# Longer visits for the projections of an RWKV-7 layer, and longer readiness times in its TensorE plan

## The chip, the cores and the metric

The kernel runs on one NeuronCore of a Trainium2 chip. The metric is the time of one execution on the device in microseconds (us), the median of several runs. Engines are named as the profile names them: PE is TensorE (matrix products), DVE is VectorE, ACT is ScalarE, POOL is GpSimd, and SP is SyncE, whose queue issues most of the DMA loads.

## The reference

A trunk of two layers over one sequence of 256 tokens and 1024 channels, all float32. Layer 0 mixes tokens by a bidirectional RWKV-7, layer 1 by dilated windowed attention; each is followed by a mixture of 32 experts of which a token uses two. The change lies in the RWKV layer, cut here to what matters:

```python
xs = h[:, :, None, :] + xx[:, :, None, :] * mu
rkv = jnp.einsum('bsjd,jde->bsje', xs[:, :, :3], w_rkv)      # r, k, v: 1024 x 1024 each
...
def step(state, inp):                                        # 16 heads of 64, two directions
    r_t, w_t, k_t, v_t, a_t, b_t = inp
    sa = jnp.einsum('bhvk,bhk->bhv', state, a_t)
    state = (state * w_t[:, :, None, :] + sa[:, :, :, None] * b_t[:, :, None, :]
             + v_t[:, :, :, None] * k_t[:, :, None, :])
    return state, jnp.einsum('bhvk,bhk->bhv', state, r_t)
...
y = (y - mean) * lax.rsqrt(var + RWKV_GN_EPS) * heads(ln_w) + heads(ln_b)
o = jnp.sum(heads(g) * (y + bonus), axis=0).reshape(bsz, s, d)
return jnp.einsum('bsd,de->bse', o, w_o)
```

## The kernel before

The RWKV layer works on blocks of 128 channels, that is two heads: eight blocks, i from 0 to 7. The sequence is cut into four chunks of 64 tokens, and the scan is turned into products within and between chunks. A block goes through these steps, each a generator whose `yield`s mark places where TensorE may turn to something else:

- `project` (L788): `keys` (L732) forms k and r (PE tile `kr`, 8 products each over the 8 blocks of input channels), `values` (L769) forms v (tile `v`, 8 products), `rates` (L747) the decay and the learning rate (tiles `ss` and `L`, then four tanh on ScalarE, L764, which empty the two `L` banks), `centred` the centred v (`vc`). The PSUM tiles of all of these, and of `yT`, `gT`, `ada` and the first half of `wo`, take turns in the two banks of the pool `pp`.
- `scale_keys` (L813) and `chunks` (L872): the decay sums, the products within chunks (`G`, masked on VectorE at L885), transposes (`BT`), `R2` and `sT`. At its end the block is "ready". The `project` of block i begins only when block i - 2 is "ready" (L790).
- `inverse` (L934): a 64 x 64 triangular inverse for each head, chunk and direction, in half precision (PE tile `iv`): six levels, each level two groups of 16 small products with a mask on VectorE (L979) or copies on ScalarE (L957) between them. Its first products are `iv<-cst,X`, its last `iv<-Q,E`.
- `recur` (L1015): four steps from chunk to chunk. A step is R (product with the state SD, an addition on VectorE at L1031), U (a product, copied on ScalarE at L1041), S (products, scaled into the new state SD on VectorE at L1057) and Y (the output, copied on ScalarE at L1073).
- `finish` (L1109): the normalisation on VectorE (with the reciprocal root in lines 345 to 354), the transposes `yT`, ScalarE's `yn` (L1124), the gate `gT` and the sum.

Beside them run `modulation_flow` (L1161), which forms the adaLN columns of later layers from streamed `aring` tiles (VectorE `acc`, L376; PE `ada`), and `outputs`, the output projection (`wo`): its first half (16 products over blocks 0 to 3) when block 7 is projected and block 3 is finished, its second half when the inverse of block 7 is done.

`weave` (L277) writes the order of the whole stage at build time, before anything runs. It keeps a time of its own. Each stream has a rank (`RANK`, L33: recurrence first, then inverse, ada, finish, chunks, supply of projections, outputs) and a time at which it may go on. `weave` takes the stream of the best rank whose time has come, advances its own time by an estimate of the products that it issued (`pe_work`) plus 0.12 where there were any, and lets the stream wait by the number that its `yield` gives. These numbers, the readiness times, stand for the work of VectorE and ScalarE until the next product has its data:

```python
ripe = [s for s in free if s[2] <= now]
s = min(ripe, key=lambda v: RANK[v[1]]) if ripe else min(free, key=lambda v: v[2])
...
r = next(s[0], "end")
...
used = pe_work[0] - before
now += used + (0.12 if used else 0.0)
s[2], s[3] = (now, r) if callable(r) else (now + (r or 0.0), None)
```

TensorE then executes its products in that order (`on_pe`, L261), and the other engines get priorities from the same time. The weights come through one SP queue: `wring` tiles of 128 x 2048 (two in the beginning), `aring` tiles of 128 x 1024 (two). When block 7 is projected and the ada columns are done, `releases` (L1280) frees the memory of the mixed inputs and of `aring` for four more `wring` tiles, then more when block 7 is ready, inverted and recurred; these fill with the first expert layer's weights.

Of the kernel before, what the change touches and what calls it, by code (L numbers as in the profile page):

```python
# [234 lines left out]
def trunk(ctx, tc, names, aps, out, stages=("rwkv", "moe0", "attn", "moe1"), dbg=None, ring=2):  # L235
# [12 lines left out]
    def bank(name="ps", tag="ps"):  # L248
        return psum[-1][tag].tile([128, 512], F32, name=name, tag=tag)
# [9 lines left out]
    pe_work, pinned = [0.0], [False]  # L259
# [77 lines left out]
    def col(i, n=1):  # L337
        t, i = (cols, i) if i < N_COLS else (cst_rw[0], i - N_COLS)
        return t[:, i:i + n]
# [243 lines left out]
    def rwkv(pool):  # L583
# [121 lines left out]
        def after(*what):  # L705
            return lambda: all(w in done for w in what if w[1] >= 0)
# [18 lines left out]
        def half(i):  # L725
            return slice(64 * i, 64 * i + 64)
# [5 lines left out]
        def keys(i):  # L732

            kr = stream.take(("kr", i)).rearrange("p (j k n) -> p j k n", j=2, k=KD)
            ps = bank(name="kr", tag="pp")
            for j, xs in enumerate((xk, xr)):
                for k in range(KD):
                    mm(ps[:, j * S:(j + 1) * S], kr[:, j, k, :], xs[k], start=(k == 0), stop=(k == KD - 1))
                    if k % 2:
                        yield  # L740
            krT = sup.tile([128, 2, S], F32, name="krT")
            A.activation(out=krT.rearrange("p j t -> p (j t)"), in_=ps, func=AF.Copy)
            sq = sup.tile([128, S], F32, name="ksq", bufs=1)
            A.activation(out=sq, in_=krT[:, 0], func=AF.Square, scale=col(C_KK + i))
            ws[i] = dict(sq=sq, kT=krT[:, 0], rT=krT[:, 1])
# [23 lines left out]
        def values(i, w):  # L769

            wv = w["vl"][:, 0:1024].rearrange("p (k n) -> p k n", k=KD)
            ps = bank(name="v", tag="pp")
            for k in range(KD):
                mm(ps[:, 0:S], wv[:, k, :], xv[k], start=(k == 0), stop=(k == KD - 1))
                if k % 2:
                    yield
            w["vT"] = sup.tile([128, S], F32, name="vT")
            A.activation(out=w["vT"], in_=ps[:, 0:S], func=AF.Copy)
# [9 lines left out]
        def project(i):  # L788

            yield after(("ready", i - 2))  # L790
            yield from keys(i)
            w = ws[i]
            w["vl"] = stream.take(("vl", i))
            yield
            yield from values(i, w)
            w["wait"] = 0.0
            g = rates(i, w)
            next(g)
            yield 0.2
            centred(i, w)  # L800
            yield 0.5
            for _ in g:
                yield
            done.add(("project", i))
# [67 lines left out]
        def chunks(i, w):  # L872
# [5 lines left out]
            for z in range(2):  # L878
                pair = [bank(name="G") for _ in range(2)]
                for c in range(4):  # L880
                    for hh, ps in enumerate(pair):
                        mm(ps[:, c * 128:(c + 1) * 128], BK[half(hh), z, c, :], AR[half(hh), z, c, :])
                for hh, ps in enumerate(pair):
                    for o, t in ((0, GV), (64, GI)):
                        V.tensor_tensor(out=t[:, z, hh].rearrange(aq, q=2),  # L885
                                        in0=ps.rearrange("p (a q n) -> p a q n", a=2, q=2)[:, :, :, o:o + 64],
                                        in1=mk[:, z, :, o:o + 64].unsqueeze(1).to_broadcast([128, 2, 2, 64]),
                                        op=ALU.mult)
                yield 1.6

            gv = GV.rearrange("p z h c n -> p (z h) c n")
            Ah, Al = A16[2 * (i % 2):2 * (i % 2) + 2]
# [122 lines left out]
        def recur(i, w):  # L1015
# [6 lines left out]
            for s in range(4):  # L1022
                cz = (s, 3 - s)
                if s == 0:
                    R = R2[:, 0]
                else:
                    R = odd.tile([128, 2, 64], F32, name="R", bufs=2)
                    ps = bank(name="R1", tag="ch")
                    for z in range(2):
                        mm(ps[half(1 - cz[z] % 2), 0:128], AR[:, z, cz[z], 0:64], ST[:, z, :])  # L1030
                    V.tensor_tensor(out=R, in0=ps[:, 0:128].rearrange("p (h n) -> p h n", h=2), in1=R2[:, s],  # L1031
                                    op=ALU.add)
                    yield 0.65
                ps = bank(name="U", tag="ch")
                for hh in range(2):
                    for z in range(2):
# [6 lines left out]
                if s < 3:  # L1043
# [16 lines left out]
                    pe_s = pe_work[0]  # L1060
# [12 lines left out]
                    A.activation(out=YT[h, z, cz[z] // 2, :], in_=py[h, 0:128], func=AF.Copy)  # L1073
                if s < 3:
                    ST = Sn
                    yield max(0.1, 0.9 - (pe_work[0] - pe_s))
                if s == 1:
                    done.add(("half", i))
            done.add(("recur", i))
# [29 lines left out]
        def finish(i, w):  # L1109
# [4 lines left out]
            sq = sub.tile([128, 8, 64], F32, name="gsq", bufs=1)  # L1114
            rs = head_scale(y, sq, 8)
            V.tensor_tensor(out=y, in0=y, in1=rs.unsqueeze(2).to_broadcast([128, 8, 64]), op=ALU.mult)
            yield 5.0
            ps = bank(name="yT", tag="pp")
            for z in range(2):
                for a in range(2):  # L1120
# [1 line left out]
                    tr(ps[:, o:o + 128], w["YT"][:, z, a, :])  # L1122
            y = sub.tile([128, 512], F32, name="yn", tag="gsq", bufs=1)
            A.activation(out=y, in_=ps, func=AF.Identity, scale=col(C_LNW + i), bias=col(C_LNB + i))  # L1124
            yield 0.1
            P.tensor_tensor(out=y, in0=y, in1=sT, op=ALU.add)
            V.tensor_tensor(out=y, in0=y, in1=w["gate"] if i == 6 else gate(i), op=ALU.mult)
            P.tensor_tensor(out=oT[:, i], in0=y[:, 0:S], in1=y[:, S:2 * S], op=ALU.add)
# [104 lines left out]
        for _ in keys(0):  # L1233
            pass
# [822 lines left out]
```

## Time and profile before

| | us |
|---|---|
| runs | 1192.64, 1196.88, 1201.08 |
| median | 1196.88 |
| the profiled execution's own time | 1199.42 |
| its span, first to last instruction | 1197.6 |
| PE busy | 1032.7 (86%) |
| DVE busy | 630.1 (53%) |
| ACT busy | 426.5 (36%) |

The span is what the trace covers; the profiled execution took 1.8 us more. Times in the rows below count from the start of the span. Busy times of PE are modelled, since products overlap. A float32 product stands in the trace as two records, so that `x4` in a timeline row is two blocks of a projection. Idle time in the trace is put down to the instruction that ended last of those waited for. PEclk is the clock that the chip granted to TensorE as a share of 2.4 GHz.

### The profile page before, as it was taken

The page shows a single profiled execution, that of the slowest core. Times are in us where ns is not written, and L with a number is a line of the kernel's source. Part 1 is how long each engine was busy: PE and PEld are TensorE (multiplying, and loading weights), DVE is VectorE, ACT ScalarE, POOL GpSimd, SP SyncE. Part 2 cuts the span into 40 slices and gives each one's busy share as a digit, 9 for nine tenths or more (in the row PEclk, how much of TensorE's full clock was granted, in tenths as well). Part 3 has the DMA queues.
Part 4 walks back from the last instruction along what each step waited for, and adds up shares of the span by engine and source line. Part 5 has one row for each costly group of instructions (what it writes and reads, how often), then busy time and mean ns, then how long its engine had stood idle before and what let it go on. Part 6 is the DMA issues. An engine that isn't in the chain of part 4 may idle for free. (4 is left out here: it accounts for less than half of the span.)

```text
span 1197.6 us, 24990 instructions
## 1 busy us (share of the span) xinstructions
PE 1032.7 (86%) x10564; PEld 689.1 (58%) x10564; DVE 630.1 (53%) x1438; ACT 426.5 (36%) x907; POOL 169.7 (14%) x122
## 2 busy tenths in 40 slices
PE   4769888989988999979988799898979999799876
PEld 3657666766666655434442388777858754344422
DVE  6873867577584446312211468987884762121112
ACT  3324456356446342101000367555544521010011
POOL 4410001010102700000000112122283000000000
PEclk8669999899979899989999999998989999899989
DMA  9453425234232766898999987876754589989995
GB/s 368 147 198 128 138 84 179 70 131 147 89 129 91 298 266 257 364 419 357 420 421 420 422 340 266 313 269 261 246 177 141 211 351 383 418 357 421 421 421 216
DMA packets 53197, 322.01 MB, mean 269 GB/s; under 512 B 5922, under 2 KB 6562, under 8 KB 21458
## 3 DMA queue, kind: packets, MB, share of 16 engines
q1 hardware_dynamic: 51986, 315.88, 67.8%
q0 software_dynamic: 800, 3.36, 0.7%
q8 instruction: 87, 1.43, 0.5%
q10 hardware_dynamic: 288, 1.05, 0.3%
q14 instruction: 36, 0.29, 0.1%
HBM read 319.22 MB, written 1.05 MB: 267 GB/s over the span
## 5 line engine op out<-in xcount | busy, mean ns | idle before, releaser
L271 PE MATMUL gu<-wring,xT 128*32 128x512 f32 x1024 | 132.2, 617 | 18.5 <-DMA wring<-in_w_moe_dram 11.2
L376 DVE SCALAR_TENSOR_TENSOR acc<-aring,silu,acc 128x512 f32<-128x512 f32 x140 | 115.0, 852 | 23.6 <-DMA aring<-in_w_ada_dram 23.3
L443 POOL TENSOR_TENSOR wl<-wring,wh 128x1024 f16<-128x1024 f32 x24 | 56.3, 2349 | 414.5 <-DMA wring<-in_w_qkv_dram 262.7
L271 PE MATMUL qkv<-hh,wl 128*128 128x256 f16 x384 | 106.7, 278 | 2.8 <-DVE wl L449 2.8
L271 PE MATMUL qkv<-hl,wh 128*128 128x256 f16 x384 | 106.6, 278 | 2.0 <-DVE hl L1720 2.0
L271 PE MATMUL qkv<-hh,wh 128*128 128x256 f16 x384 | 106.7, 278 | 1.6 <-ACT hh L1719 1.6
L271 PEld LDWEIGHTS gu<-wring,xT 128*32 128x32 f32 x1024 | 30.9, 112 | 101.9 <-issue 79.8
L271 PEld LDWEIGHTS <-wh 128*128 128x128 f16 x768 | 76.7, 100 | 13.3 <-issue 3.6
L271 PE MATMUL dn<-wring,hidT 128*32 128x256 f32 x1024 | 66.7, 410 | 18.1 <-ACT hidT L1522 18.1
L449 DVE SCALAR_TENSOR_TENSOR wl<-wring,wh 128x1024 f16<-128x1024 f32 x56 | 71.2, 1276 | 16.7 <-ACT wh L445 16.6
L271 PE MATMUL acc<-y,back 128*128 128x512 f32 (+1 forms) x144 | 65.9, 581 | 10.3 <-DVE y L1549 8.1
L271 PEld LDWEIGHTS xT<-oh,x 128*128 128x128 f32 x512 | 59.0, 192 | 21.1 <-issue 9.2
L445 ACT ACTIVATE wh<-wring 128x1024 f16<-128x1024 f32 x56 | 58.6, 1050 | 33.8 <-PE qkv L271 28.5
L1324 DVE SCALAR_TENSOR_TENSOR sg<-sg,gu 128x256 f32<-128x256 f32 x16 | 6.7, 420 | 118.2 <-ACT sg L1323 118.2
L1549 DVE TENSOR_TENSOR y<-dn,ga 128x512 f32<-128x512 f32 x28 | 19.4, 691 | 89.6 <-PE dn L271 60.4
L271 PE MATMUL xT<-oh,x 128*128 128x128 f32 x512 | 63.5, 280 | 2.5 <-DVE oh L1433 2.5
L271 PEld LDWEIGHTS dn<-wring,hidT 128*32 128x32 f32 x1024 | 32.3, 116 | 48.7 <-ACT hidT L1522 22.2
L1323 ACT ACTIVATE sg<-gu 128x256 f32<-128x256 f32 x16 | 6.1, 383 | 147.4 <-PE gu L271 147.4
L271 PE MATMUL qkv<-wl,hh 128*128 128x256 f16 x192 | 54.0, 281 | 0.0
L271 PE MATMUL qkv<-wh,hh 128*128 128x256 f16 x192 | 54.0, 281 | 0.0
L271 PE MATMUL qkv<-wh,hl 128*128 128x256 f16 x192 | 53.9, 281 | 0.0
L1465 ACT ACTIVATE back<-bT 128x256 f32<-128x256 f32 x16 | 6.2, 384 | 131.9 <-PE acc L271 131.9
(341 smaller groups left out, 2120.5 us busy)
## 6 DMA issues: line engine op xcount, KB each, us to landing
wring<-in_w_moe_dram SPq DMA_DIRECT2D x192, 1024.0 KB, 19.8
aring<-in_w_ada_dram SPq DMA_DIRECT2D x96, 512.0 KB, 4.5
wring<-in_w_qkv_dram SPq DMA_DIRECT2D x36, 1024.0 KB, 9.2
wring<-in_w_kr_dram SPq DMA_DIRECT2D x8, 1024.0 KB, 4.9
wring<-in_w_vl_dram SPq DMA_DIRECT2D x8, 640.0 KB, 4.8
wring<-in_w_rwo_dram SPq DMA_DIRECT2D x4, 1024.0 KB, 6.8
wring<-in_w_ato_dram SPq DMA_DIRECT2D x4, 1024.0 KB, 7.1
x<-in_x_dram POOLq DMA_DIRECT2D x2, 512.0 KB, 7.3
```

Of the source, the lines that this page charges most:

```text
L271: return on_pe(nc.tensor.matmul(out=o, lhsT=lhsT, rhs=rhs, start=start, stop=stop, **kw))
L376: V.scalar_tensor_tensor(out=acc[:, s], in0=w[:, s], scalar=silu[:, k:k + 1], in1=acc[:, s], op0=ALU.mult, op1=ALU.add)
L443: eng.tensor_tensor(out=lo, in0=src, in1=hi, op=ALU.subtract)
L445: A.activation(out=hi, in_=src, func=AF.Copy, scale=by)
L449: V.scalar_tensor_tensor(out=lo, in0=src, scalar=by, in1=hi, op0=ALU.mult, op1=ALU.subtract)
L1323: A.activation(out=o, in_=ps[:, 0:256], func=AF.Tanh, scale=0.5)
L1324: V.scalar_tensor_tensor(out=o, in0=o, scalar=1.0, in1=ps[:, 0:256], op0=ALU.add, op1=ALU.mult)
L1465: A.activation(out=back, in_=ps[:, 0:S], func=AF.Copy)
L1549: V.tensor_tensor(out=y, in0=py[c], in1=gates[i, 5][:, c * 512:(c + 1) * 512], op=ALU.mult)
```

## The change

Four kinds of lines change, and nothing of what is computed:

- `keys` and `values` offer TensorE to others after every fourth block of input channels instead of every second.
- `project` waits 1.6 after its start condition.
- Seven readiness times grow: between the parts of `chunks` 1.6 becomes 2.4; in `recur` the time behind R 0.65 becomes 0.85 and the time behind Y 0.9 becomes 1.1; in `finish` 5.0 becomes 7.0 ahead of `yT` and 0.1 becomes 1.2 ahead of `gT`.

```diff
             for j, xs in enumerate((xk, xr)):
                 for k in range(KD):
                     mm(ps[:, j * S:(j + 1) * S], kr[:, j, k, :], xs[k], start=(k == 0), stop=(k == KD - 1))
-                    if k % 2:
+                    if k % 4 == 3:
                         yield
...
                 mm(ps[:, 0:S], wv[:, k, :], xv[k], start=(k == 0), stop=(k == KD - 1))
-                if k % 2:
+                if k % 4 == 3:
                     yield
...
         def project(i):

             yield after(("ready", i - 2))
+            yield 1.6
             yield from keys(i)
...
-                yield 1.6
+                yield 2.4
...
-                    yield 0.65
+                    yield 0.85
...
-                    yield max(0.1, 0.9 - (pe_work[0] - pe_s))
+                    yield max(0.1, 1.1 - (pe_work[0] - pe_s))
...
-            yield 5.0
+            yield 7.0
             ps = bank(name="yT", tag="pp")
...
-            yield 0.1
+            yield 1.2
             P.tensor_tensor(out=y, in0=y, in1=sT, op=ALU.add)
```

The numbers steer `weave`, so the order of TensorE's products changes through the whole stage. Three places show how. In the rows that follow, the number at the start is the place in the engine's order, and x gives how many equal instructions stand in a row. First TensorE in the recurrence of block 0, before:

```order
765 L271 MATMUL kr<-xr,wring 128x256 x2
766 L271 MATMUL U<-R,TT 64x64 x4
767 L271 MATMUL R_1315<-vc,GV 64x64 x16
768 L271 MATMUL sT<-bb,cstr 128x256 x2
769 L271 MATMUL S<-SD_359,cst 64x128 x2
770 L271 MATMUL S<-UV,BT 64x64 x4
771 L271 MATMUL Y<-SD_359,AR 64x128 x2
772 L271 MATMUL Y<-UV,GI 64x64 x4
773 L271 MATMUL kr<-xr,wring 128x256 x2
774 L271 MATMUL R_1359<-SD_360,AR 64x128 x2
```

And the same place of the recurrence now (`R<-vc,GV` is the product R2 of block 1):

```order
758 L271 MATMUL v<-xv,wring 128x256 x4
759 L271 MATMUL U<-R,TT 64x64 x4
760 L271 MATMUL R_1330<-vc,GV 64x64 x16
761 L271 MATMUL sT<-bb,cstr 128x256 x2
762 L271 MATMUL S<-SD_359,cst 64x128 x2
763 L271 MATMUL S<-UV,BT 64x64 x4
764 L271 MATMUL Y<-SD_359,AR 64x128 x2
765 L271 MATMUL Y<-UV,GI 64x64 x4
766 L271 MATMUL v<-xv,wring 128x256 x4
767 L271 MATMUL R_1380<-SD_360,AR 64x128 x2
```

The visits between the steps hold four blocks instead of two, and the projection of block 2 is further on: it is at v instead of r. Second, TensorE behind the rate products of block 4, before:

```order
2558 L271 LDWEIGHTS Ah_355
2559 L271 MATMUL iv<-T_3138,Ah_355 64x64
2560 L271 MATMUL L<-hidw,wring 128x256 x2
2561 L271 MATMUL L<-hida,wring 128x256 x2
2562 L271 MATMUL kr<-xk,wring 128x256 x2
2563 L271 LDWEIGHTS X_3140
```

Now the rate products of block 4 stand at 2126, and the first visit to the projection of block 5 at 2434:

```order
2125 L275 MATMUL BT<-cst,BK 128x128 x4
2126 L271 MATMUL L<-hidw,wring 128x256 x2
2127 L271 MATMUL L<-hida,wring 128x256 x2
2128 L271 LDWEIGHTS E_2739
...
2433 L271 MATMUL iv<-T_3022,Ah_355 64x64
2434 L271 MATMUL kr<-xk,wring 128x256 x4
```

The next projection no longer follows at once; the rows between are those of the inverse (a weight load and a product each), the chunks and the recurrence. Third, SP's queue from the load of block 6's v weights to the first expert weights, before:

```order
36 L153 DMA wring<-in_w_vl_dram 128x1280
37 L153 DMA aring<-in_w_ada_dram 128x1024 x4
38 L153 DMA wring<-in_w_kr_dram 128x2048
39 L153 DMA aring<-in_w_ada_dram 128x1024 x4
40 L153 DMA wring<-in_w_vl_dram 128x1280
41 L153 DMA aring<-in_w_ada_dram 128x1024 x2
42 L153 DMA wring<-in_w_rwo_dram 128x2048 x4
43 L153 DMA wring<-in_w_moe_dram 128x2048 x45
```

And now:

```order
34 L153 DMA wring<-in_w_vl_dram 128x1280
35 L153 DMA aring<-in_w_ada_dram 128x1024 x2
36 L153 DMA wring<-in_w_kr_dram 128x2048
37 L153 DMA aring<-in_w_ada_dram 128x1024 x6
38 L153 DMA wring<-in_w_vl_dram 128x1280
39 L153 DMA wring<-in_w_rwo_dram 128x2048
40 L153 DMA aring<-in_w_ada_dram 128x1024 x2
41 L153 DMA wring<-in_w_rwo_dram 128x2048
42 L153 DMA aring<-in_w_ada_dram 128x1024 x4
43 L153 DMA wring<-in_w_rwo_dram 128x2048 x2
44 L153 DMA wring<-in_w_moe_dram 128x2048 x45
```

The last six ada loads have moved behind all the projections' weights and between the loads of the output weights. From the transposes `zT` behind the last RWKV outputs on, TensorE's order is the same in both kernels.

## Rows read from the trace of the kernel before

**Rows 1.** Stage windows: PE, PEld, DVE, ACT, POOL busy us (xinstructions), PEclk, DMA share, GB/s
```profile
95.00:415.00 320.00, 287.34 (x4461) 216.33 (x4459) 207.62 (x524) 160.46 (x355) 52.13 (x42) 0.94 0.38 131
415.00:481.00 66.00, 60.54 (x731) 35.30 (x731) 33.64 (x126) 21.78 (x58) 1.99 (x2) 0.98 0.67 264
481.00:680.00 199.00, 172.17 (x1393) 78.02 (x1386) 40.23 (x99) 23.58 (x70) 0.00 (x0) 0.97 0.98 406
```

**Rows 2.** Waits of PE from 95 to 415: total us, times, longest us
```profile
PE kr L271 <- ACT at L764: 5.4, 4, 1.7
PE R L271 <- DVE SD L1057: 3.8, 5, 1.1
...
PE yT L275 <- DVE rsq L352: 2.7, 1, 2.7
PE U L271 <- DVE R L1031: 2.1, 4, 1.0
...
PE yT L275 <- DVE rsq L353: 1.7, 1, 1.7
PE gT L271 <- ACT yn L1124: 1.7, 3, 0.7
...
PE yT L275 <- ACT at L764: 0.8, 1, 0.8
```

**Rows 3.** Timeline of PE: start us, us, engine, line, product, shape, xcount [idle before]
```profile
103.18 1.13 PE L271 MATMUL kr<-xr,wring 128*128 128x256 f32 x4
104.24 0.44 PE L271 MATMUL iv<-T,Ah 64*64 64x64 f16 x16
104.61 1.99 PE L271 MATMUL kr<-xr,wring 128*128 128x256 f32 x8
106.53 0.44 PE L271 MATMUL iv<-Q,X 64*64 64x64 f16 x16
106.81 0.42 PE L271 MATMUL iv<-X,Q 64*64 64x64 f16 x16
```

**Rows 4.** Timeline of PE, the start of a projection at 161
```profile
161.31 1.13 PE L271 MATMUL kr<-xk,wring 128*128 128x256 f32 x4 [1.73 <-ACT at L764]
```

**Rows 5.** Timeline of ACT, the tanh of line 764 ahead of it
```profile
160.80 0.47 ACT L764 ACTIVATE at<-L,a0h 128x256 f32<-128x256 f32 x1
```

**Rows 6.** Timeline of PE, steps of the inverse and the recurrence in the tail
```profile
424.23 0.44 PE L271 MATMUL iv<-Q,X 64*64 64x64 f16 x16
...
425.57 0.44 PE L271 MATMUL iv<-T,Ah 64*64 64x64 f16 x16 [0.28 <-ACT T L957]
...
426.79 0.44 PE L271 MATMUL iv<-Q,X 64*64 64x64 f16 x16 [0.52 <-DVE Q L979]
...
441.09 1.12 PE L271 MATMUL wo<-wring,oT 128*128 128x512 f32 x2
442.14 0.45 PE L271 MATMUL U<-R,TT 64*64 64x64 f32 x8
442.96 0.63 PE L271 MATMUL S<-UV,BT 128*64 128x64 f32 x8 [0.37 <-ACT UV L1041]
...
444.38 0.44 PE L271 MATMUL R<-SD,AR 128*64 128x128 f32 x4 [0.55 <-DVE SD L1057]
445.29 0.45 PE L271 MATMUL U<-R,TT 64*64 64x64 f32 x8 [0.47 <-DVE R L1031]
```

**Rows 7.** Short windows around falls of the clock, columns as in rows 1
```profile
205.00:209.00 4.00, 4.00 (x41) 2.96 (x40) 3.69 (x7) 2.38 (x5) 2.10 (x2) 0.57 0.07 26
248.00:252.00 4.00, 2.60 (x22) 1.52 (x22) 4.00 (x16) 3.12 (x7) 0.00 (x0) 0.72 0.79 269
326.00:330.00 4.00, 4.00 (x80) 3.36 (x77) 0.95 (x2) 2.95 (x8) 0.00 (x0) 1.00 0.01 4
332.00:340.00 8.00, 5.27 (x73) 4.48 (x70) 6.03 (x28) 4.27 (x10) 0.34 (x1) 0.50 0.45 133
```

**Rows 8.** Window from the first expert load to the first expert product, columns as before
```profile
385.00:481.00 96.00, 85.97 (x1071) 53.33 (x1073) 50.19 (x161) 34.67 (x84) 23.45 (x18) 0.95 0.69 274
```

## The prediction, made before the changed kernel ran

> **What bounds the kernel now.** I read the stage windows first. They cut the span where the code cuts it: the woven RWKV stage, its tail up to the first expert product at 480.8 us, the first expert layer, and the rest [rows 1]. In the expert layer the DMA share is 0.98 at 406 GB/s, while TensorE is idle for 27 of 199 us: the layer runs at the pace of its weights, and it ends a fixed time after it starts. The program from the last RWKV output on stands in the same order in both kernels, so the change is worth what it moves the start of the expert layer by, and nothing else.
>
> Before that start the DMA has room (0.38), VectorE is busy for 207.6 of 320 us and ScalarE for 160.5. TensorE is busy for 287.3 of 320, and takes its products strictly in the order that the planner wrote. So its time there is made of four things: the products, what a change from one kind of product to another costs, the waits (320.0 - 287.3 = 32.7 us), and the clock, whose mean of 0.94 over 320 us means that some 19 us of full clock are missing. The waits of TensorE then say which of them come from an order that is too early for its data [rows 2]: kr on the tanh that frees its bank 5.4 us, yT on the normalisation 2.7 + 1.7 + 0.8 = 5.2, R on the state 3.8, U on R 2.1, gT on yn 1.7. These five make 18.2 us, and five of the change's longer readiness times stand just there. They add no wait to any instruction: they only move it back in TensorE's order.
>
> **A: fewer visits.** Both kernels execute the same products. A visit of two blocks takes from 103.18 to 104.24, which is 1.06 us to the next product; one of four takes from 104.61 to 106.53, 1.92 us [rows 3]. Two visits of two cost 2.12, so each visit that goes saves 0.20 us. The inverse step beside it takes 0.37 us when a projection follows (104.24 to 104.61) and 0.28 when another inverse step follows (106.53 to 106.81), so up to 0.09 more. In the order there are 78 visits by kr and v from block 1 on before (six of them of four blocks already) and 42 after: 36 x 0.20 = 7.2 us, at most 36 x 0.29 = 10.4, and nothing if TensorE only waits longer instead. I take -7.2, as TensorE is 90% busy.
>
> **B: waits that are aimed at.** The wait for the bank: kr stands at 161.31 after 1.73 us of idle, and the tanh that releases the bank starts at 160.80 and takes 0.47, so it ends at 161.27 [rows 4, 5]. The added 1.6 us ahead of a projection covers all but about 0.1 of each such wait: -5.0. The 5.0 that became 7.0 covers the two shorter yT waits and 2.0 of the longest: -4.5. For gT 0.1 became 1.2, more than any of its three waits: -1.7. R gets 0.2 more on each of 5 waits, -1.0; U 0.2 on each of 4, -0.8. Sum -13.0. The lower bound is -18.2, all of it; the upper is 0, if no product is ready to stand in the gap. I take -13.0 because a planner that holds a product back puts another stream's product there, and through most of the stage there is one. The sixth, in the chunks, meets none of the larger waits [rows 2]; I cost it at nothing, as inverse and recurrence products fill it. Without them it would cost the 0.8 that it adds, 6.4 us over eight blocks.
>
> **C: new waits.** Fewer, larger pieces of projection run out sooner. After block 4's last rate product the order before goes straight on to the next projection; the new order has some 300 rows of inverse and recurrence in between, since block 5 has to wait for "ready" of block 3. Such windows follow blocks 4, 5, 6 and 7, and one stands at the end of the first output half: five. What a wait costs there, the tail shows. With no filler at all one recurrence step lasts from 442.14 to 445.29, of which 0.37 + 0.55 + 0.47 = 1.39 us are waits; where inverse and recurrence alternate, 425.57 to 426.79 has 0.28 + 0.52 = 0.80 [rows 6]. High end: all four steps bare in five windows, 4 x 5 x 1.39 = 27.8 us. Low end 0. In the new order the two chains alternate in these windows, as they do in the second of these rows, so I take 5 x 0.80 = +4.0.
>
> **D: output products that move.** With the projections gone earlier, 12 instead of 5 of the first output's blocks stand ahead of the last block's inverse, and 4 instead of 11 inside it. Seven times 1.05 us (441.09 to 442.14 [rows 6]) = 7.4 us are paid earlier and leave the tail. Whether the tail gives them back depends on what they hid there: products of the inverse behind copies on ScalarE and masks on VectorE. That inverse runs from 415 to 442 with its outputs in it; without seven of them it would take 19.5 us. An inverse step waits for its mask at least until 1.22 us after the product ahead of it (425.57 to 426.79), and the half of a level that goes through ScalarE takes 1.34 (424.23 to 425.57): five levels are 12.8 us, by estimate, which leaves 6.7 us for its first and last parts, unbounded by these rows. So much of it can come back. The bounds are 0 and +7.4; I take about half, +3.4.
>
> **E: the clock.** The clock falls to its lower level, 1.2 GHz, in stretches. Two of them follow waits that B removes: 205 to 209 at 0.57, behind waits of yT and gT, and 248 to 252 at 0.72, in the wait of kr [rows 7]. They lose 4 x 0.43 + 4 x 0.28 = 2.8 us, and I take -2.8. But the longest fall, at 0.50 from 332 on, follows a stretch in which TensorE was busy for 4.00 of 4.00 us. The Trainium skill ("TensorE: Matmul & The Clock Gate", the section "HAM oscillation — how this bites in real kernels") puts such falls down to gaps in which the engine waits; by it, removing waits would bring back most of the 19 us and the sum would be some 16 us lower. The trace agrees at 205 and 248 and not at 330, so that is a rival below. The bounds are -19 (full clock throughout) and +20 (five windows of 8 us at half clock, each losing 4, the size of the row from 332 to 340).
>
> **What hides the rest.** The queue of loads has the projections' weights behind other ada loads than before (six ahead of the last vl). Before, too, a run of six stands ahead of one projection load, and TensorE shows no wait for a DMA in the stage; the DMA share of 0.38 [rows 1] is the cover. If it went, v would wait for its load of 128 x 1280 floats, 0.66 MB or 1.6 us at the expert layer's 406 GB/s. A shorter stage loads VectorE more: 207.6 us of work over about 305 is 68%, still cover.
>
> **The sum.** -7.2 - 13.0 + 4.0 + 3.4 - 2.8 = -15.6 us. The profiled execution took 1199.4 us (span 1197.6 and 1.8 around it), so 1183.8; it lies 2.5 us above the median of 1196.9, which makes **1181**.
>
> **The rivals.**
> Waits only move (0.20). Each product held back leaves a gap, or what stands in it makes the next chain late. B and E are then 0, and -7.2 + 4.0 + 3.4 is 0.2: 1197. For it: the longer waits are in the planner's own time, and most waits end on VectorE or ScalarE, whose speed doesn't change. Against it: 5.4 us hang on one bank at a fixed delay.
> The clock holds (0.12). With few waits the clock stays at 2.4 GHz: E is -19, the sum -31.8: 1165. For it the falls at 205 and 248, against it the one from 332.
> The weights come late (0.06). The extra ring space for expert weights opens after the last ada product, which stood some 300 rows of the order ahead of the last inverse and now stands some 40 ahead of it. Up to 481 the queue brought in 96 x 274 = 26.3 MB [rows 8], 65 us at the expert layer's 406 GB/s; from the start of the last inverse to the expert layer there were 66 us, and will be some 62. With two gaps of 4 us the layer starts 8 us short of weights: 1189.
> Fillers run out: slower (0.12). All windows of C are bare, 27.8, the clock falls in each, +20, and the outputs give nothing back, +7.4: with A and B +35 us, 1232. It decides from the point at which C, D and E together exceed 20 us for slower at all, 32 for slower by over 1%. For it: the new order's long rows of small products; against it: alternating chains at 425 hardly waited.
>
> **How the numbers follow.** A measurement of this kernel tells about 1% (12 us) from no change. My forecast has 0.50; its own range is 1173 to 1190, and 0.40 of the 0.50 lies below 1185. Faster: 0.40 + 0.12 = 0.52. Within 1%: 0.10 + 0.20 + 0.06 = 0.36. Slower: 0.12. The range from 1165 to 1198 takes in the clock's rival and the one in which waits only move, and leaves out the slow case and a little beyond the other end.
>
> **What would show it.** Right: the kr wait on the tanh near 0.5 us in all, yT and gT nearly gone, four-block visits of about 1.92 us, the first expert product near 465 us and the expert layer still 199 us long. Wrong in C: waits of R, U and S above 12 us in all. Wrong in D: a last inverse that still takes 25 us. Wrong in E: a mean clock below 0.92 ahead of the tail. Wrong as a whole: a first expert product later than 480, or an earlier one with an expert layer longer by as much.

## The result, and the profile after

The changed kernel takes 1203.1 us (median; 1196.5 to 1209.2) where the kernel before took 1194.6 on the same chip. The ratio is 1.0076 with a 95% interval from 1.0049 to 1.0103: slower by three quarters of a per cent, where 1.3% faster was predicted. One of the eleven executions took 5376.42 us and counts in neither the spread nor the ratio. The profiled execution took 1209.15 us (span 1207.4), 9.7 us more than that of before; it is the longest of the other ten, so its rows show one to three microseconds more than the median loses.

First the stage windows of the changed kernel, with the columns of [rows 1], cut at the same events: the last inverse's start, the first expert product (492.06 us, where the prediction named "later than 480" as its sign of being wrong as a whole) and the end of the first expert layer.

```profile
95.00:424.00 329.00, 290.70 (x4471) 222.91 (x4469) 217.57 (x523) 158.37 (x353) 51.25 (x42) 0.92 0.38 127
424.00:492.00 68.00, 58.09 (x721) 35.48 (x715) 33.47 (x126) 22.43 (x60) 1.98 (x2) 0.90 0.66 255
492.00:691.00 199.00, 172.64 (x1387) 77.80 (x1388) 40.42 (x100) 23.19 (x68) 0.00 (x0) 0.95 0.98 404
```

The expert layer lasts 199 us, as in [rows 1], and starts 11.3 us later (480.80 before). So the loss lies where the prediction looked for the gain. One window over the whole stage, of the kernel before and then of the changed one, splits it:

```profile
95.00:480.80 385.80, 347.68 (x5185) 251.48 (x5183) 241.06 (x648) 182.24 (x413) 54.13 (x44) 0.95 0.43 154
```

```profile
95.00:492.06 397.06, 348.78 (x5184) 258.39 (x5182) 251.10 (x648) 180.80 (x413) 53.23 (x44) 0.92 0.42 149
```

TensorE is idle for 397.06 - 348.78 = 48.3 us instead of 38.1, so 10.2 of the 11.3 us are waits. Its busy time did not fall by the 7 us of the saved visits; the granted clock is 0.92 instead of 0.95 in the same stretch. And VectorE, with the same 648 instructions, is busy 10 us longer. That last number points at the cause, but does not measure the loss: the visits alone, which are faster than before, have it too (250.3 us of VectorE up to their first expert product). The waits of TensorE in the same stretch, to be held against [rows 2]:

```profile
PE iv L271 <- DVE T L999: 10.6, 3, 6.8
PE R L271 <- DVE SD L1058: 6.4, 7, 2.3
PE iv L271 <- DVE Q L980: 5.7, 8, 1.9
PE U L271 <- ACT TT L1012: 4.2, 3, 2.2
...
PE S L271 <- ACT UV L1042: 2.2, 2, 1.8
...
PE U L271 <- DVE R L1032: 0.8, 1, 0.8
PE yT L275 <- DVE YT L1117: 0.6, 1, 0.6
```

Three of the five waits that the change aimed at are gone: kr 5.4 to nothing (1.7 us of the wait for that bank now stand at an ada product), gT 1.7 to nothing, yT 5.2 to 0.6. Of the other two, U on R fell from 2.5 to 0.8 and R on the state rose from 4.3 to 6.4 (the values of before up to 480.8 us). The largest is a new one, for T of line 999, which VectorE makes at the end of each inverse; before, TensorE did not wait for it at all. Here is the longest of the three, on TensorE, then VectorE, then POOL, each a timeline of the changed kernel:

```profile
401.93 0.44 PE L271 MATMUL iv<-X,E 64*64 64x64 f16 x16
409.14 0.64 PE L271 MATMUL iv<-X,cst 64*64 64x512 f16 x2 [6.77 <-DVE T L999]
```

```profile
397.01 0.42 DVE L886 TENSOR_TENSOR GV<-G,cstr 128x256 f32<-128x256 f32 x1 [0.84 <-PE G L271]
...
400.17 0.69 DVE L1128 TENSOR_TENSOR yn<-yn,gT 128x512 f32<-128x512 f32 x1 [1.73 <-POOL yn L1127]
408.06 0.43 DVE L899 TENSOR_TENSOR Ah<-Ah,cst 128x512 f16<-128x512 f16 x1 [7.21 <-POOL Al L898]
408.41 0.68 DVE L999 TENSOR_TENSOR T<-iv,E 128x512 f16<-128x512 f32 x1
```

```profile
395.18 3.73 POOL L566 TENSOR_TENSOR wring<-wring,ga 128x512 f32<-128x512 f32 x3
398.86 1.27 POOL L1127 TENSOR_TENSOR yn<-yn,sT 128x512 f32<-128x512 f32 x1
400.09 4.94 POOL L566 TENSOR_TENSOR wring<-wring,ga 128x512 f32<-128x512 f32 x4
404.97 1.15 POOL L898 TENSOR_TENSOR Al<-GV,Ah 64x512 f16<-64x512 f32 x1
406.08 0.72 POOL L1129 TENSOR_TENSOR oT<-yn 128x256 f32<-128x256 f32 x1
406.88 1.15 POOL L898 TENSOR_TENSOR Al<-GV,Ah 64x512 f16<-64x512 f32 x1
```

Read from the bottom: POOL gates the rows of the output projection, 16 multiplications of 1.23 us or more each (L566, called by `outputs`). `Al` of block 7 stands behind them. VectorE takes its instructions in the order of these rows: the addition to `Ah` waits 7.21 us for `Al`, and T of block 6's inverse, which does not read that `Al`, stands behind `Ah`. TensorE waits 6.77 us for T. In VectorE's order of the changed kernel `Ah` stands ahead of the running inverse's T in three of eight blocks, in the kernel before in none. That was theory 1.

### The profile page after: what moved, and what is told of

It is laid out like the page before. It is cut to its first block, busy times and chain, and to the rows that moved or that the text cites. A ratio compares the mean times of both kernels' runs of the same rounds, so it can differ in the third digit from the quotient of the medians.

```text
span 1207.4 us, 24980 instructions
## 1 busy us (share of the span) xinstructions
PE 1035.4 (86%) x10564; PEld 697.1 (58%) x10564; DVE 641.7 (53%) x1438; ACT 424.2 (35%) x907; POOL 168.5 (14%) x122
## 3 DMA queue, kind: packets, MB, share of 16 engines
q10 hardware_dynamic: 288, 1.05, 0.3%
HBM read 319.22 MB, written 1.05 MB: 265 GB/s over the span
## 5 line engine op out<-in xcount | busy, mean ns | idle before, releaser
L566 POOL TENSOR_TENSOR wring<-wring,ga 128x512 f32<-128x512 f32 x32 | 45.6, 1454 | 64.2 <-DMA wring<-in_w_rwo_dram 34.8
```

Of the source, the lines that this page charges most:

```text
L566: P.tensor_tensor(out=wk[:, j, s], in0=wk[:, j, s], in1=gate[:, s], op=ALU.mult)
```

## The experiments

Every ratio is against the kernel before, run beside it on the same chip, in five rounds; the intervals are of 95%. One table first, as the pieces are read against each other. "Gate moved" takes the 16 multiplications off POOL, "Al moved" the two subtractions per block.

| Order of TensorE | POOL as it is | gate moved | Al moved | both moved |
|---|---|---|---|---|
| before | 1 | 1.0014 (e9) | 0.9896 (e5) | 0.9931 (e12) |
| visits only | 0.9929 (e1) | 0.9940 (e14) | 0.9933 (e7) | |
| project wait only | 1.0087 (e8) | 0.9994 (e10) | | |
| all readiness times, no visits | 1.0037 (e2) | | | |
| visits and project wait | 1.0115 (e6) | | | |
| changed, without project wait | 0.9955 (e4) | | 0.9948 (e16) | |
| changed, finish times of before | | 0.9989 (e15) | | |
| changed | 1.0076 | 0.9980 (e11) | 0.9967 (e3) | 0.9922 (e13) |

### First set: which half, and is it T?

e1 has the visits alone (`k % 4 == 3` in `keys` and `values`), e2 the readiness times alone (the other lines of the diff), and e4 is the changed kernel without one of them:

```diff
             yield after(("ready", i - 2))
-            yield 1.6
             yield from keys(i)
```

e3 is the changed kernel with Al moved:

```diff
-                P.tensor_tensor(out=l, in0=a, in1=h, op=ALU.subtract)
+                V.tensor_tensor(out=l, in0=a, in1=h, op=ALU.subtract)
```

> Edit: the kernel before with only the two visit sizes changed (four blocks of channels), all readiness times as before. In its order VectorE has the next block's addition to Ah ahead of the El of the running inverse in three of the eight inverses (none in the kernel before). Theory 1 (the larger visits bring the next block's chunks forward, and their VectorE and POOL work then stands in in-order queues ahead of the end of the running inverse): the waits of TensorE for the DVE tile T of L998 come back, 6 us or more in sum, and what the saved switches give (7 us) is lost again: 1.000 to 1.010 times before. Rival 2 (the readiness times do the harm, the visits are worth what was predicted): 0.993 to 0.997, with those waits near 0.

Measured: 0.9929 [0.9901, 0.9958]. The waits for T were 3.6 us, neither the 6 of theory 1 nor the 0 of rival 2, and the visits alone are worth what the prediction's term A said. The time is at the lower edge of rival 2's, and theory 1's count of `Ah` ahead of T does not decide: this kernel has three as well.

> Edit: the kernel before with only the readiness times changed (all six), visits of two blocks as before. Its VectorE order has no Ah ahead of an El. Theory 1 (visits bring the chunks forward): the waits for the DVE tile T are 0, the aimed-at waits kr, yT and gT are gone as in the changed kernel, and the time is 0.990 to 1.000 of before. Rival 2 (the readiness times do the harm, through waits of R, U and S and a lower clock where the fillers were used up): 1.005 to 1.013, with the waits of R, U and S over 12 us as in the changed kernel.

Measured: 1.0037 [1.0015, 1.0060], between the two. kr is gone and no wait for T appears, and yT still has 1.7 us and gT 0.5; but iv on Q takes 10.1 us in place of 3.6, and iv on ACT's T 6.8 in place of 1.9.

> Edit: the changed kernel with the subtraction Al (two instructions per block) moved from POOL to VectorE, so that the addition to Ah has no wait for POOL in VectorE's queue. Theory 1: the waits of TensorE for the DVE tile T fall from 10.6 us to under 4 us, and with the clock that falls after them the time is 6 to 12 us under the changed kernel's, 0.997 to 1.003 of before. Rivals 2 and 3 (R, U and S waits, or the clock where fillers lack): the waits for T may fall, but the time stays within 3 us of the changed kernel's, 1.005 to 1.010 of before.

Measured: 0.9967 [0.9942, 0.9992], 1.1% under the changed kernel; the waits for T fell from 10.6 to 4.3. That is close to what theory 1 asked for (under 4), but a control was missing.

> Edit: the changed kernel without the readiness time of 1.6 ahead of project; visits of four blocks and the other five times stay. In its VectorE order no Ah stands ahead of an El. Theory 1: the waits for the DVE tile T are near 0, the wait for the bank at the first product of a block comes back (kr or ada, up to 5 us), and the time is 0.993 to 1.001 of before. Rival 2 (the other readiness times do the harm): still 1.004 to 1.010. Rival 4 (the late start of project alone does it, by delaying the chain): 0.985 to 0.995, by more than the waits for T explain.

Measured: 0.9955 [0.9932, 0.9979]. Taking one readiness time back is worth 1.2%, within theory 1's range; the waits for T are 3.0 us in this profile and kr's 0.8.

### Second set: the control, and the wait ahead of project

e5 is the kernel before with Al moved, e7 the visits with Al moved; e6 has the visits and the wait ahead of project; e8 only that wait.

> Control: the kernel before with the two Al subtractions of each block moved from POOL to VectorE, as in the run on the changed kernel (which that move made 1.1% shorter). Theory 1 (there the move helped because Ah waits for POOL ahead of the end of a running inverse; here every inverse has ended by then, so the 18.8 us that VectorE waits for POOL in this kernel keep TensorE from nothing): 0.997 to 1.004 of before. Rival 5 (the move is worth something in any order, since Al on POOL is slow and late): 0.985 to 0.992.

Measured: 0.9896 [0.9857, 0.9934]. Rival 5 holds: the move is worth as much in the kernel before as in the changed one, so e3 says nothing of the change. By its ratio it is the shortest kernel of this study, below before and changed alike; its interval overlaps those of e13 and the kernels around 0.993. The 18.8 us that VectorE waited for Al there stood ahead of the next inverse's first mask; TensorE's idle time fell by 4.8 us (38.1 to 33.3), though its list of waits never named POOL.

> Edit: the kernel before with the four-block visits and the wait of 1.6 ahead of project; the other five readiness times as before. Theory 6 (the wait ahead of project and the large visits act together: a project that starts a turn late and then comes in large pieces pushes the next block's chunks into the end of the running inverse or the recurrence): 1.002 to 1.010 of before, 0.9% or more over the visits alone (0.9929). Rival 2 (chunks, recurrence and finish times do the harm, or only all six together): 0.990 to 0.997. In VectorE's order two of its inverses have Ah ahead of El; three in the changed kernel, three with the visits alone.

Measured: 1.0115 [1.0077, 1.0152], the longest of all, from two edits that were each meant to help. TensorE waits 14.9 us in five times for YT at yT, and 6.49 us once for Q; the section on the prediction comes back to the second.

> Edit: the kernel before with the four-block visits, and Al moved to VectorE. With the visits alone the waits of TensorE for the tile T were 3.6 us (two) and the time 0.9929. Theory 1: most of these 3.6 us and the late X of block 7 (VectorE waits 6.5 us for POOL there) are saved: 0.986 to 0.992, the shortest so far. Rival 7 (the visits alone have no POOL wait on the path, so the move only loads VectorE with 14 instructions more): 0.992 to 0.997.

Measured: 0.9933 [0.9904, 0.9962]. With the visits the move gives nothing, as rival 7 has it.

> Edit: the kernel before with only the readiness time of 1.6 ahead of project. The prediction's term for the waits kr (5.0 us of the 13.0) says 0.995 to 0.997 with the wait of kr for tanh (5.4 us in four) gone. Theory 6 (the wait harms only with the large visits): the kr wait goes, 0.996 to 1.002. Rival 8 (the wait harms by itself, since a block of products less lies between the chain's steps at its start): 1.003 to 1.010, with other waits of 5 us or more in kr's place.

Measured: 1.0087 [1.0056, 1.0119]. Rival 8, with theory 6 refuted: the wait of 1.6 harms by itself, and term B had given it 5.0 us of gain. kr's wait is gone, and others stand in its place, 14.5 us in two instructions. This kernel has no `Ah` ahead of a T, so theory 1 cannot be the cause. Its trace shows another. TensorE's two long waits:

```profile
380.23 1.22 PE L271 MATMUL vc<-cstr,vT 128*128 128x128 f32 x4 [5.75 <-DVE kss L753]
...
401.25 0.80 PE L271 MATMUL G<-AR,BK 64*128 64x128 f32 x4 [8.80 <-DVE BK L846]
```

VectorE ahead of each (e8; the second number is the duration of the instruction):

```profile
372.41 1.19 DVE L345 TENSOR_SCALAR rsy<-gvar 128x8 int32<-128x8 int32 x1
373.52 0.16 DVE L347 TENSOR_SCALAR rsh<-gvar 128x8 f32<-128x8 f32 x1
373.64 1.19 DVE L348 TENSOR_TENSOR rsq<-rsy 128x8 f32<-128x8 f32 x1
...
378.52 1.19 DVE L352 TENSOR_TENSOR rsq<-rsy 128x8 f32<-128x8 f32 x1
379.74 0.17 DVE L353 TENSOR_TENSOR rsq<-rsq,rsh 128x8 f32<-128x8 f32 x1
379.94 0.17 DVE L354 SCALAR_TENSOR_TENSOR rsy<-rsq,rsy 128x8 f32<-128x8 f32 x1
380.02 0.15 DVE L753 TENSOR_SCALAR kss<-ss 128x4 f32<-128x4 f32 x1
...
392.18 1.48 DVE L853 TENSOR_TENSOR AR<-kk,eb 128x256 f32<-128x256 f32 x1
...
401.12 1.48 DVE L846 TENSOR_TENSOR BK<-kd,e 128x256 f32<-128x256 f32 x1
402.52 0.41 DVE L846 TENSOR_TENSOR BK<-bb,e 128x256 f32<-128x256 f32 x1
```

And POOL in the same time:

```profile
371.09 8.59 POOL L566 TENSOR_TENSOR wring<-wring,ga 128x512 f32<-128x512 f32 x7 [14.21 <-DMA wring<-in_w_rwo_dram]
...
390.44 11.88 POOL L566 TENSOR_TENSOR wring<-wring,ga 128x512 f32<-128x512 f32 x8
```

VectorE does not wait; its instructions are longer. All but one of the steps on 128x8 numbers take 1.05 to 1.19 us while POOL multiplies (371.09 to 379.68), and 0.17 from the moment POOL has finished; a product of 128x256 takes 1.48 until 402.3 and 0.41 behind it. POOL's own multiplications take 11.88 / 8 = 1.49 us there, and 8.59 / 7 = 1.23 in the first batch, beside the small steps. The first batch starts when the load of the output weights has landed (POOL was idle for 14.21 us until then). It makes the small steps of `finish` late, `kss` of block 7 stands behind them, so `scale_keys` of block 7 starts 6 us late and runs into the second batch. The Trainium skill ("SBUF — State Buffer", the section "Who interferes with whom") states the rule: a VectorE instruction with two inputs in SBUF and a GpSimd instruction that reads SBUF contend for a shared port, and whichever starts first keeps it for its whole instruction. The trace agrees: 0.41 becomes 1.48.

I summed this for each trace: for every form of VectorE instruction in the stage the time above its median (instructions over 0.3 us above it), put down to the POOL instruction beside it. All of it lies beside one. Total, and the part beside L566, in whole microseconds (the texts below have 8.6 where this count gives 8.1 and 7.8):

| | before | changed | e1 | e6 | e8 | e10 | e11 |
|---|---|---|---|---|---|---|---|
| excess of VectorE, us | 7 | 15 | 15 | 18 | 20 | 6 | 8 |
| beside L566, us | 1 | 8 | 8 | 13 | 15 | 0 | 0 |

In the kernel before, the two batches run from 376.3 to 381.2 and from 393.3 to 409, and block 7's `scale_keys` from 386 to 394: it fits between them. That is theory 9.

In the changed kernel the gate acts in two ways. The 8 us beside L566 lie between 346 and 371 us; around the wait of 6.77 us (396 to 409) no instruction of VectorE is longer than elsewhere, and there the gate only keeps POOL from `Al`, as shown above. In e8 `Al` is done before the gate starts (354.50 to 356.88), so only the longer instructions are left.

### Third set: the gate off POOL

The rows of the output projection are no longer multiplied by the gate; the sums are, in PSUM, which is the same product. TensorE's order stays as it is.

```diff
-                w = gated(stream.take(("rwo", 0, c)), gates[0, 2][:, c * 512:(c + 1) * 512], 4)
+                w = stream.take(("rwo", 0, c))
...
+                    V.tensor_tensor(out=ps, in0=ps, in1=gates[0, 2][:, c * 512:(c + 1) * 512], op=ALU.mult)
                     add_out(ps, t, c)
...
-            blocks = [gated(b, gates[0, 2], 2).rearrange("p (k n) -> p k n", k=2)
+            blocks = [b.rearrange("p (k n) -> p k n", k=2)
...
+            V.tensor_tensor(out=po[b], in0=po[b], in1=gates[0, 2][:, b[1] * 512:(b[1] + 1) * 512], op=ALU.mult)
             add_out(po[b], *b)
```

> Edit: the kernel before without the 16 multiplications by which POOL gates the rows of the output projection (1.23 us each, L566); VectorE multiplies the eight finished sums in PSUM by the same gate instead (about 0.7 us each, four of them behind the last product). TensorE's order is the same. Theory 9 (a VectorE instruction that meets a POOL instruction takes up to 1 us longer: 128x8 steps 1.19 instead of 0.16 us): in this kernel only 1.0 us of VectorE's excess lies under these multiplications, though Al of block 7 waits behind them (8.95 us of VectorE): 0.992 to 1.000. Rival 6 (the order alone decides, POOL does not matter): 1.000 to 1.004, for the four multiplications at the end.

Measured: 1.0014 [0.9990, 1.0038]. In the order of before the move is worth nothing (rival 6's range, which allows for the four multiplications that it adds at the end).

> Edit: the kernel with only the readiness time of 1.6 ahead of project (1.0087 of before), now without POOL's 16 gate multiplications, as in the run beside it. There 15.2 us of VectorE's excess lay under them, and TensorE waited 5.75 us for kss and 8.80 us for BK. Theory 9: both waits go, 0.993 to 1.001 of before, within 0.4% of the kernel before with the same edit. Rival 6 (the late projects cost by the order they give): 1.004 to 1.010, still 0.8% over the kernel before with the same edit.

Measured: 0.9994 [0.9971, 1.0017], 0.93% under e8 with the same order of TensorE. Theory 9's range holds and rival 6's does not: with TensorE's order unchanged, the loss of e8 comes from the gate on POOL. The same steps of VectorE in e10:

```profile
372.25 0.17 DVE L345 TENSOR_SCALAR rsy<-gvar 128x8 int32<-128x8 int32 x1
372.33 0.17 DVE L347 TENSOR_SCALAR rsh<-gvar 128x8 f32<-128x8 f32 x1
372.45 0.17 DVE L348 TENSOR_TENSOR rsq<-rsy 128x8 f32<-128x8 f32 x1
...
373.74 0.15 DVE L753 TENSOR_SCALAR kss<-ss 128x4 f32<-128x4 f32 x1
...
385.22 0.41 DVE L853 TENSOR_TENSOR AR<-kk,eb 128x256 f32<-128x256 f32 x1
```

`kss` is 6.3 us earlier, the wait of vc for it is gone, G's waits on BK are 2.3 us instead of 11.0, the last inverse starts at 407.0 instead of 422.7 and the expert layer at 479.6 instead of 491.5.

> Edit: the changed kernel (1.0076 of before) without POOL's 16 gate multiplications. There VectorE had 8.6 us of excess with them, and Ah of block 7 waited 7.21 us for Al, which stood behind them on POOL. Theory 9: the waits of TensorE for T fall from 10.6 to under 5 us, and the time to 0.992 to 1.000 of before, within 0.4% of the kernel before with the same edit. Rival 6: 1.003 to 1.009.

Measured: 0.9980 [0.9952, 1.0008], 0.96% under the changed kernel. The place shown above is now

```profile
397.57 0.44 PE L271 MATMUL iv<-X,E 64*64 64x64 f16 x16
398.12 0.40 PE L271 MATMUL iv<-X,cst 64*64 64x512 f16 x2
```

```profile
397.05 0.43 DVE L899 TENSOR_TENSOR Ah<-Ah,cst 128x512 f16<-128x512 f16 x1 [2.58 <-POOL Al L898]
```

with VectorE's wait for `Al` 2.58 instead of 7.21 us; the waits for T are 3.9 us in all. The last inverse starts at 408.1 instead of 424.1, the expert layer at 476.2 instead of 492.1. So theory 1's row was right as a row, but what made it long was the gate ahead of `Al` on POOL. The run takes away both ways in which the gate acts here and so does not say how much each cost.

> Edit: the kernel before with both moves, Al to VectorE and the gate to the sums in PSUM, so that POOL keeps only two additions of finish per block in this stage. Theory 9: the two gains overlap (each frees Al of block 7), so 0.984 to 0.990, at or a little below Al alone (0.9896). Rival 6: 0.989 to 0.994, Al alone plus the four multiplications at the end.

Measured: 0.9931 [0.9900, 0.9962], no shorter than Al alone; the gains do not add (rival 6's range).

### Fourth set: what is still missing of the predicted gain

e13 is the changed kernel with both moves, e14 the visits with the gate moved, e15 the changed kernel with the gate moved and `finish` at 5.0 and 0.1 as before, e16 is e4 with Al moved.

> Edit: the changed kernel with both moves (Al to VectorE, gate to the sums in PSUM). Beside it stand the kernel before with both moves (0.9931 of before) and the changed kernel with the gate alone moved (0.998). Theory 9 (all that the change loses lies in meetings of VectorE and POOL): the predicted 1.3% appears, 0.980 to 0.988. Rival 10 (the waits for R, U, Q and X that the new order makes eat the rest): 0.990 to 0.997, no shorter than the kernel before with both moves.

Measured: 0.9922 [0.9891, 0.9953], against 0.9931 for the kernel before with both moves. With POOL out of the way the change is worth nothing that can be measured: rival 10.

> Edit: the four-block visits alone (0.9929 of before), without POOL's gate. There 8.6 us of VectorE's excess lay under the gate multiplications at 343 to 369 us. Theory 9: 0.985 to 0.991, and the readiness times are then worth nothing or a loss (changed kernel with the same edit: 0.998). Rival 11 (what lies under the multiplications there is off the path): 0.992 to 0.996.

Measured: 0.9940 [0.9912, 0.9969]. The 8 us that VectorE loses beside L566 with the visits alone (e1) were off the path (rival 11). So a meeting costs only on some chains; in e8 it was the one that TensorE waited for.

> Edit: the changed kernel without POOL's gate (0.998) and with finish's readiness times of before (5.0 and 0.1). Seven products of the output projection stand ahead of the last inverse's start in its order, where the changed kernel has twelve and the kernel before five. Term D of the prediction (products moved ahead of the last inverse cost half of 7.4 us): 0.992 to 0.996, 3 us or more under the run without the gate, less what the waits for yT bring back (2 to 5 us). Rival 12 (the products' place costs nothing): 0.998 to 1.003.

Measured: 0.9989 [0.9960, 1.0017] against 0.9980: no difference. It is inconclusive for term D, since the waits for yT came back as 8.7 us in its profile, more than the 2 to 5 expected. What it does show is that `finish`'s longer times, which remove these 8 us of waits, are worth nothing in sum with the order that they bring.

> Edit: the changed kernel without the readiness time ahead of project (0.9955 of before) and with Al on VectorE: the shortest combination in sight. If the gains add: 0.984 to 0.990. If Al was off the path there, as with the visits alone (0.9929 and 0.9933 with it): 0.993 to 0.997.

Measured: 0.9948 [0.9922, 0.9974], as if Al had not been moved (0.9955).

## Why the prediction was wrong

Two steps failed: the cover in "What hides the rest", which made the difference between no loss and a loss, and term B, without which no gain is left but that of the visits. (The change has six readiness times, five that grow and the new 1.6; the "seven" ahead of the prediction is a miscount.)

**The cover.** The prediction has VectorE with 68% of load as "still cover". It read the share of load, not what VectorE meets on POOL, and did not use the POOL column of [rows 1] (52 us in 42 instructions) at all. A sum over TensorE's order cannot see that block 7's chain slides into POOL's batches: its small steps beside them in e8, its `Al` behind them in the changed kernel. With the gate moved, the changed kernel is shorter by 0.96% of before and e8 by 0.93%, and the kernel before is not shorter (1.0014): this is the whole loss against before, about half of the way from the predicted 0.987 to the measured 1.0076.

**B, the waits aimed at (-13.0).** Three of the five waits went, the time did not. (One reading was wrong: the yT wait of 0.8 us in [rows 2] ends on the tanh of line 764, so it is for a bank and not for the normalisation.) The wait ahead of project, 5.0 us of the term, measured 1.0087 (some 10 us of loss) and, with the gate off POOL, 0.9994 against 1.0014: about 2 us of gain, within the intervals. `finish`'s times, 6.2 us of it, measured nothing in e15. All the times together, with the gate moved, are 0.9980 against 0.9940 for the visits alone: no gain. The step that failed is "a planner that holds a product back puts another stream's product there", as far as it was to give time back. With the gate moved in both, TensorE is idle for 37.9 us up to the expert layer in the order of before (e9) and for 39.7 in the changed one (e11): kr, yT and gT are gone, while Q went from 3.8 to 6.2, U on `TT` from 0.5 to 4.2 and T from nothing to 3.9. That the chains held back are late themselves is a reading of these rows; no run tests it by itself. This was the rival "waits only move", for which the prediction had 0.20 and 1197; with POOL's gate moved the changed kernel comes out near it (0.9980).

**A, fewer visits (-7.2).** Right. A visit of four takes 1.92 us, as [rows 3] had it:

```profile
101.24 1.99 PE L271 MATMUL kr<-xk,wring 128*128 128x256 f32 x8
103.16 0.44 PE L271 MATMUL iv<-T,Ah 64*64 64x64 f16 x16
```

The visits alone measured 0.9929, 8.5 us (5 to 12), though this order also moves the outputs that D has at +3.4. It is the only part of the change that was measured as a gain.

**C, new waits (+4.0).** Its own test fails: R, U and S wait 6.4 + 4.2 + 0.8 + 2.2 = 13.6 us, over the 12 named. The same view of before has 9.5 (R 4.3, U 2.5 and 0.5, S 2.2), so the growth, 4.1, has the size of the term. But the larger new waits are elsewhere: T 10.6 for nothing, Q 5.7 for 3.6.

**D, moved outputs (+3.4).** The last inverse takes 26.1 us (424.12 to 450.20), where 25 was to show the term wrong; before it took 26.9 (415.26 to 442.14). So the tail gave back almost nothing of the 7.4. TensorE is busy for 20.8 of these 26.1 us, before for 25.9 of 26.9, and the clock fell in the inverse's last part; first the changed kernel, then the one before:

```profile
440.00:450.20 10.20, 6.25 (x155) 4.95 (x154) 4.24 (x16) 4.18 (x8) 0.41 (x1) 0.70 0.76 308
```

```profile
436.00:441.20 5.20, 5.20 (x119) 2.98 (x114) 1.89 (x3) 1.68 (x3) 1.10 (x2) 1.00 0.22 91
```

And the move belongs to the visits: e1 has eleven blocks ahead of the last inverse as well, and is faster. Whether they cost anything in the whole is not shown: no run moves them alone, and e15 could not tell.

**E, the clock (-2.8).** The sign was wrong: 0.92 instead of 0.94 up to the last inverse's start and 0.90 instead of 0.98 in the tail. The mean over whole runs is 0.933 in ten runs of the changed kernel, 0.942 in 30 of the kernel before, and 0.948 in six of e5. But e1, at 0.932, is faster than before, so the clock alone does not decide the order of the kernels; no run changes it by itself.

What stays open is how much of e6, the longest, is due to the gate: it was not run without it. Its trace shows the rows of e8 again, with 13 us of excess beside L566. POOL's second batch, the VectorE products beside it, and TensorE's wait for the Q behind them:

```profile
385.42 17.19 POOL L566 TENSOR_TENSOR wring<-wring,ga 128x512 f32<-128x512 f32 x12 [9.50 <-DMA wring<-in_w_rwo_dram]
```

```profile
391.59 1.48 DVE L846 TENSOR_TENSOR BK<-bb,e 128x256 f32<-128x256 f32 x1
392.99 0.68 DVE L980 TENSOR_TENSOR Q<-iv,cst 128x512 f16<-128x512 f32 x1
```

```profile
393.72 0.64 PE L271 MATMUL iv<-Q,X 64*64 64x64 f16 x16 [6.49 <-DVE Q L980]
```

## What to carry to other kernels

A readiness time that removed a wait on TensorE moved later chains on the other engines too; try each such number alone, since here one of six cost 0.9% and hid the 0.7% that the visits gained. Before calling an engine cover, compare the duration of one form of its instructions beside a busy POOL and away from it: a stretched instruction shows as busy, and the lists of TensorE's waits here named VectorE, never POOL. Work on POOL that can go elsewhere (Al to VectorE: 1.0% by one line) is worth a run even where nothing seems to wait for POOL.

## What the hardware showed

The contention goes in both directions. In the kernel before, POOL is the loser: an addition that takes 1.27 us elsewhere takes 3.35 while VectorE runs seven products back to back at their usual length (389.46 to 392.1):

```profile
389.93 3.35 POOL L1126 TENSOR_TENSOR yn<-yn,sT 128x512 f32<-128x512 f32 x1 [8.69 <-ACT yn L1124]
```

And an instruction of VectorE with one of its two inputs in PSUM was not held: in the changed kernel GV from G (397.01) takes 0.42 us and yn from gT (400.17) 0.69, both beside POOL's multiplications and no longer than elsewhere. One-input TENSOR_SCALARs on 128x8 numbers were held in e8 (1.05 and 1.19 us) as well as passed (0.16), which these runs leave unexplained.
